# Late first stage: modulation steps moved into the feed-forward, convolution totals in place, taps and splits queued behind evacuations

## The chip, the cores and the metric

The kernel runs on one core of a Trainium2 chip. Its time is the device time of that core in microseconds. A core has TensorE (PE, matrix products), VectorE (DVE), ScalarE (ACT), GpSimd (POOL), SyncE (SP, whose queue issues the weight transfers here) and 16 DMA engines. Each engine works through a queue of its own in order; an instruction whose input or buffer is not ready holds up everything behind it on that engine.

## The reference

Two transformer blocks for 512 positions of width 1024, in fp32. The part that matters is the first block:

```python
h = rmsnorm(x, norm1_g)
z_glu, z_rx, z_rg, z_ga, z_gb = jnp.split(h @ w_in + b_in, split_idx, axis=-1)
u = z_glu[..., :1024] * sigmoid(z_glu[..., 1024:])
u = causal_depthwise_conv(u, conv_dw_w, conv_dw_b)           # 31 taps, 1024 channels
u = silu(layernorm(u, conv_ln_g, conv_ln_b))
y_a = u @ conv_w_out + conv_b_out
xb = causal_depthwise_conv(z_rx, lru_conv_w, lru_conv_b)     # 4 taps, 1280 channels
hb = rg_lru(xb, ...)                                         # gates, linear recurrence
y_b = (hb * gelu(z_rg)) @ lru_w_out
m = sigmoid(z_ga) * y_a + sigmoid(z_gb) * y_b
x = x + m @ w_mix_out
h = rmsnorm(x, norm2_g)
x = x + (silu(h @ ffn_w1) * (h @ ffn_w3)) @ ffn_w2           # then rmsnorm, then the second block
```

The second block starts from `mods = silu(c) @ w_ada + b_ada`: 9216 numbers from a 1024 x 9216 matrix, which depend on `c` alone and are first needed when the second block scales its input.

## The kernel before

Channels lie on the 128 partitions, the 512 positions along the free axis, so an activation is a list of tiles of 128x512. Every operand of a product is split into a high and a low fp32r part, and every product of a weight tile and an activation tile is three matmuls (`mm3`, L132 to L134: high x high, high x low, low x high). A weight block (512 KB, 128x1024) comes by DMA on SP's queue into one of 5 buffers `st`; ScalarE makes its high part `whi` (L125), VectorE or POOL its low part `wlo` (L126), 5 buffers each. Inside the first stage two of three low parts go to POOL. A product of 8 weight tiles (24 matmuls) is called a gemm below. Its result lies in one of 3 PSUM buffers `mm`; 5 more, `ax`, hold the accumulators of the convolution and small sums.

The program is a list of steps, each with its weights, a function and a slack, the time that its matmuls leave to the other engines. After each step, background work (`bg`) is queued until the slack is used up (`runbg`), and `defer(n, f)` queues `f` some gemms later. So the numbers of slack and cost decide where in the queues of VectorE and ScalarE a piece of background work stands. `tc.issue_after(x)` places instructions behind `x` in the queue.

The order of the first stage is written out: `g0 r0 r1 r2 r3 r4 g1 g2 a0 r5 a1 g3 a2 r6 a3 g4 a4 r7 r8 s0 g5 r9 b0 g6 b1 b2 g7 b3 b4`, then ten `q` with `s1`, then 8 `yb`, 8 `ga`, 8 `ya`, `mix`, and the feed-forward.

- `g` (`glu_step`): two gemms into `ga` (evacuated by ScalarE at L421) and `th` (evacuated at L430, multiplied at L431). The result is convolved in the background: 31 taps into two accumulators in PSUM, the first two by ScalarE (L401 to L404), 29 by VectorE (L406), then a total (L446, L447) and POOL's running sum `lnm` (L479).
- `r` (`rx_step`): a gemm into `rx` and the four taps `xb`. The steps g0 and r0 to r4 work on the input that is not yet normalised, so VectorE multiplies their results by the norm (`raw_z`, L395, tile `rx`) while `norm_h` makes the normalised input. Work that these steps leave behind is collected in the list `late`.
- `a`, `b` (`gate_step`): products of `xb`'s high and low parts `xbh`, `xbl` into the gates; `s`: the recurrence; `q` (`rg_step`): the gelu branch, whose product with the recurrence is split into `hbh`, `hbl`.
- `yb` (two products, 54 matmuls, from `hb` and the input), `ga` (one gemm), `ya` (one gemm on `u2h`, `u2l`, the normalised convolution).
- The layer norm is background work: `ln_mean` (sum of `lnm` over the partitions on TensorE, L196; VectorE makes `dg`, L217; TensorE spreads it, L224), `ln_var` (VectorE subtracts, L639; ScalarE squares, L251; VectorE sums into `lnv`, L252), `ln_rstd` (again L196, L217, L224), `ln_out` (L646, L647 and the splits `u2h`, `u2l`).

The modulation is 72 steps `ada_step`: a 512 KB DMA of `w_ada` into an `st` buffer and one VectorE operation over 128x1024 (L327) that sums a row into `mods`. Before, they stand behind every second `yb` (4), every `ga` (8), six of the `ya` and at places behind; the last runs at 761.55 us, and the first instruction that reads `mods` for the second block starts at 860.0 us.

## Time and profile before

| | us |
|---|---|
| median of 3 runs | 2270.68 (2270.66 to 2271.85) |
| the profiled execution | 2268.78 |
| its span, first to last instruction | 2267.1 |
| TensorE busy | 2207.7 (97%) |
| VectorE busy | 1401.8 (62%) |
| ScalarE busy | 941.8 (42%) |
| POOL busy | 159.3 (7%) |
| mean granted clock of TensorE | 0.991 of 2.4 GHz |

The span covers the time between the first and the last instruction; the profiled execution's own time is 1.7 us longer. TensorE is busy nearly everywhere, so what counts is where it is not: in the first 440 us, where the page's slices of its busy time fall to 9 and once to 6 tenths.

### The profile page before, as it was taken

How to read it: one execution, taken by the hardware profiler on the slowest of the kernel's cores; microseconds unless marked ns; L12 is line 12 of the kernel's file. 1: busy time of each engine (PE TensorE's matmuls, PEld its weight loads, DVE VectorE, ACT ScalarE, POOL GpSimd, SP SyncE). 2: the span in 40 equal slices, each digit the busy share in tenths (PEclk: the TensorE clock that was granted, in tenths of full speed). 3: DMA queues.
4: the chain of work that ended last, by engine and by line, in shares of the span. 5: the costliest groups of instructions: out<-in, count | busy, mean ns of one | idle time of the engine just before them, and what ended most of it. 6: DMA issues, size and time to landing. Idle time of an engine off the chain costs nothing.

```text
span 2267.1 us, 29984 instructions
## 1 busy us (share of the span) xinstructions
PE 2207.7 (97%) x11688; PEld 1888.2 (83%) x11688; DVE 1401.8 (62%) x2349; ACT 941.8 (42%) x1517; POOL 159.3 (7%) x179
## 2 busy tenths in 40 slices
PE   8899999699999999999999999999999999999997
PEld 6687788588888899988889987888888899988887
DVE  7999996768555448433325768675656558433334
ACT  6566433443222235322224567573433445322232
POOL 3334330000000000000100011000000000000000
PEclk9999999799999999999999999999999999999999
DMA  5433347245656534423234431213222323423342
GB/s 191 118 92 122 101 134 225 82 144 174 203 195 192 150 103 149 131 94 102 86 102 129 161 96 57 66 47 103 66 75 75 117 89 96 147 95 98 92 121 66
DMA packets 81438, 265.54 MB, mean 117 GB/s; under 512 B 10208, under 2 KB 12512, under 8 KB 81296
## 3 DMA queue, kind: packets, MB, share of 16 engines
q1 hardware_dynamic: 79888, 262.64, 36.8%
q8 instruction: 92, 1.51, 0.3%
q0 software_dynamic: 1264, 0.69, 0.1%
q14 instruction: 50, 0.41, 0.1%
q10 hardware_dynamic: 144, 0.29, 0.0%
HBM read 255.13 MB, written 4.19 MB: 114 GB/s over the span
## 4 chain that ended last, share of the span: by engine, by line
PE 81%; DVE 11%; issue 1%; ACT 1%; DMA 0%; POOL 0%; DVEq 0%; ACTq 0%; POOLq 0%
PE mm L132 24%; PE mm L133 24%; PE mm L134 24%; DVE ax L406 3%; DVE wlo L126 1%; PE ax L1231 1%; PE ax L1232 1%; PE ax L1233 1%; PE ax L1286 1%; PE ax L224 1%; PE ax L1415 1%; DVE xb L406 1%; PE ax L196 1%; DVE xb L567 1%; DMA st<-w_ada 0%
## 5 line engine op out<-in xcount | busy, mean ns | idle before, releaser
L125 ACT ACTIVATE whi<-st 128x1024 fp32r<-128x1024 f32 (+3 forms) x420 | 427.1, 1018 | 959.3 <-PE mm L133 594.4
L126 DVE TENSOR_TENSOR wlo<-st,whi 128x1024 fp32r<-128x1024 f32 (+3 forms) x378 | 454.1, 1202 | 415.8 <-ACT whi L125 414.7
L132 PE MATMUL mm<-pfh,whi 128*128 128x512 f32 (+1 forms) x1676 | 568.9, 339 | 0.5 <-ACT sq L251 0.5
L133 PE MATMUL mm<-pfl,whi 128*128 128x512 f32 (+1 forms) x1676 | 565.6, 338 | 0.0
L134 PE MATMUL mm<-pfh,wlo 128*128 128x512 f32 (+1 forms) x1676 | 564.4, 337 | 1.2 <-DVE wlo L126 1.2
L134 PEld LDWEIGHTS mm<-pfh,wlo 128*128 128x128 f32 x1676 | 316.8, 189 | 34.0 <-DVE wlo L126 1.9
L132 PEld LDWEIGHTS mm<-pfh,whi 128*128 128x128 f32 x1676 | 317.2, 189 | 33.5 <-ACT sq L251 1.4
L133 PEld LDWEIGHTS mm<-pfl,whi 128*128 128x128 f32 x1676 | 317.1, 189 | 31.7 <-issue 0.5
L132 PE MATMUL mm<-hi,whi 128*128 128x512 f32 x464 | 183.0, 394 | 10.4 <-ACT hi L354 6.2
L133 PE MATMUL mm<-lo,whi 128*128 128x512 f32 x464 | 183.4, 395 | 1.3 <-DVE lo L355 1.3
L134 PE MATMUL mm<-hi,wlo 128*128 128x512 f32 x464 | 182.4, 393 | 0.4 <-DVE wlo L126 0.4
L132 PE MATMUL mm<-mh,whi 128*128 128x256 f32 (+1 forms) x528 | 176.7, 335 | 2.2 <-ACT mh L852 1.1
L133 PE MATMUL mm<-ml,whi 128*128 128x256 f32 (+1 forms) x528 | 176.9, 336 | 0.0
L134 PE MATMUL mm<-mh,wlo 128*128 128x256 f32 (+1 forms) x528 | 176.4, 334 | 0.0
L406 DVE SCALAR_TENSOR_TENSOR ax<-th,d_hdw,ax 128x508 f32<-128x508 f32 (+27 forms) x232 | 157.7, 729 | 1.1 <-ACT ax L401 0.2
L133 PE MATMUL mm<-m1l,whi 128*128 128x512 f32 x368 | 143.3, 390 | 0.2 <-DVE m1l L686 0.2
L134 PE MATMUL mm<-m1h,wlo 128*128 128x512 f32 x368 | 143.0, 389 | 0.0
L132 PE MATMUL mm<-m1h,whi 128*128 128x512 f32 x368 | 143.0, 389 | 0.0
L327 DVE SCALAR_TENSOR_TENSOR st<-st,crow 128x1024 f32<-128x1024 f32 x72 | 88.5, 1229 | 73.6 <-DMA st<-w_ada 73.5
L865 DVE TENSOR_TENSOR fs<-fs,mm 128x512 f32<-128x512 f32 (+1 forms) x75 | 45.0, 600 | 128.0 <-PE mm L134 127.7
L132 PEld LDWEIGHTS mm<-hi,whi 128*128 128x128 f32 x464 | 88.1, 190 | 29.6 <-ACT hi L354 6.2
L132 PEld LDWEIGHTS mm<-mh,whi 128*128 128x128 f32 x528 | 100.1, 190 | 13.1 <-ACT mh L852 1.5
(363 smaller groups left out, 3319.2 us busy)
## 6 DMA issues: line engine op xcount, KB each, us to landing
st<-w_gu SPq DMA_DIRECT2D x102, 512.0 KB, 3.5
st<-w_ada SPq DMA_DIRECT2D x72, 512.0 KB, 4.0
st<-ffn_w SPq DMA_DIRECT2D x56, 512.0 KB, 3.6
st<-w_in SPq DMA_DIRECT2D x51, 512.0 KB, 4.0
st<-w2fm SPq DMA_DIRECT2D x51, 512.0 KB, 3.5
st<-w_dn SPq DMA_DIRECT2D x38, 448.0 KB, 3.3
st<-w_dn SPq DMA_DIRECT2D x24, 512.0 KB, 3.6
st<-w2v SPq DMA_DIRECT2D x16, 512.0 KB, 3.5
```

The costliest lines, as they stand in the source:

```text
L125: h = act(hi, src, AF.Copy)
L126: (eng or V).tensor_tensor(lo, src, hi, ALU.subtract)
L132: mm(out, whi, xh, start=start, stop=False)
L133: mm(out, whi, xl, start=False, stop=False)
L134: block[0] = mm(out, wlo, xh, start=False, stop=stop)
L196: mm(pc[:, i * nt + j:i * nt + j + 1], acc[:, r[0] + P * j:r[0] + P * (j + 1)], ones1, start=True, stop=True)
L224: mm(R[:, :nt * P], ones, dg.rearrange("p n t -> p (n t)"), start=True, stop=True)
L327: V.scalar_tensor_tensor(w, w, 1.0, crow, ALU.mult, ALU.mult, accum_out=mods[:, n:n + 1])
L406: V.scalar_tensor_tensor(acc[:, d:], u[:, :T - d], w, acc[:, d:], ALU.mult, ALU.add)
L567: V.tensor_tensor_scan(XB[j], GT[0, j], XB[j], 0.0, ALU.mult, ALU.add)
L865: V.tensor_tensor(s, s, rs(st["u"], r), ALU.mult)
L1231: mm(o, h[:, sl], hi[c], start=k == 0, stop=False)
```

## The change

Five things are changed, all in the program of the first stage and the feed-forward.

1. The modulation steps behind `yb` and `ga` (12) are gone from there. Two more stand behind `ya`, seven more in the first feed-forward (1.2 instead of 1.0 per weight pair's half) and three more in the product after it.
2. A convolution's total is written into the tile that was convolved (`u`, tile name `th`), not into a new one (`cv`).
3. First taps, totals and splits of ScalarE are queued behind the last evacuation of a PSUM buffer (`EV`), VectorE's taps behind the second last of certain multiplies (`DV`).
4. Of the work in `late`, three pieces are queued in the last `norm_h`, the rest behind the multiply of r4 (`raw_end`).
5. The last `hb` is split one gemm earlier, the layer norm's work waits for one step less, and in `yb` the background gets 1.15 times the slack.

```diff
--- before.py
+++ after.py
@@ -363,6 +363,7 @@
+    NEARLY = 3
     late = []
 
     def norm_h(m0):
@@ -380,19 +381,23 @@
                 h, l = H["h"][m]
                 H["h_last"] = V.tensor_tensor(l, ts[m - m0], h, ALU.subtract).ins
             if m0 + 2 == KT:
-                for f in late:
+                for f in late[:NEARLY]:
                     f()
-                late[:] = [None]
+                del late[:NEARLY]
         return fn
 
     def raw_end(W):
         del H["xg"], H["R"]
+        H["h_last"] = H["z_last"]
+        for f in late:
+            f()
+        late[:] = [None]
 
     def raw_z(W, t):
 
         ps = pmm()
         gemm(ps, W, H["xg"])
-        V.tensor_tensor(t, ps, H["R"], ALU.mult)
+        H["z_last"] = V.tensor_tensor(t, ps, H["R"], ALU.mult).ins
         return t
 
     def delay(acc, u, d, w, b, first=False):
@@ -407,6 +412,16 @@
 
     CV = [None] * KT
     EV = [None]
+    DV = [None, None]
+
+    def behind_ev():
+        return tc.issue_after(EV[0].ins) if EV[0] is not None else nullcontext()
+
+    def behind_dv():
+        return tc.issue_after(DV[0].ins) if DV[0] is not None else nullcontext()
+
+    def dv(ins):
+        DV[:] = [DV[1], ins]
 
     def glu_step(m, raw=False):
         st = {}
@@ -427,8 +442,8 @@
             else:
                 pg = pmm()
                 gemm(pg, W, H["h"])
-            act(u, pg, AF.Tanh, bias=dcol["hb_in"][:, 8 + m:9 + m], scale=0.5)
-            V.scalar_tensor_tensor(u, u, 1.0, st["a"], ALU.add, ALU.mult)
+            EV[0] = act(u, pg, AF.Tanh, bias=dcol["hb_in"][:, 8 + m:9 + m], scale=0.5)
+            dv(V.scalar_tensor_tensor(u, u, 1.0, st["a"], ALU.add, ALU.mult))
             cv = {}
 
             def taps(d0, d1):
@@ -438,12 +453,14 @@
                     for d in range(d0, d1):
                         w = dcol["hdw"][:, m * 31 + 30 - d:m * 31 + 31 - d]
                         acc = cv["p"][d % 2]
-                        delay(acc, u, d, w, col("conv_dw_b", m), first=d < 2)
+                        with behind_ev() if d < 2 else behind_dv():
+                            delay(acc, u, d, w, col("conv_dw_b", m), first=d < 2)
                 return f
 
             def total():
-                CV[m] = at(n="cv")
-                act(CV[m], cv["p"][0], AF.Copy)
+                CV[m] = u
+                with behind_ev():
+                    act(u, cv["p"][0], AF.Copy)
                 V.tensor_tensor(CV[m], CV[m], cv["p"][1], ALU.add)
 
             def convolve():
@@ -510,7 +527,9 @@
 
             def parts():
                 XBP[j] = (at(F32R, "xbh"), at(F32R, "xbl"))
-                split(xb, *XBP[j])
+                with behind_ev():
+                    act(XBP[j][0], xb, AF.Copy)
+                V.tensor_tensor(XBP[j][1], xb, XBP[j][0], ALU.subtract)
 
             def sides(m):
 
@@ -542,7 +561,7 @@
                 mm3(pg, hi[2 * q], lo[2 * q], *XBP[j], True, False)
                 mm3(pg, hi[2 * q + 1], lo[2 * q + 1], *XBN[j], False, True)
                 th = at(n="gt")
-                act(th, pg, AF.Tanh, bias=dcol[nmq][:, j:j + 1], scale=0.5)
+                EV[0] = act(th, pg, AF.Tanh, bias=dcol[nmq][:, j:j + 1], scale=0.5)
                 GT[q, j] = th
             r, ith = GT[0, j], GT[1, j]
             tt = at(n="tt")
@@ -551,7 +570,7 @@
             a2 = at(n="a2")
             GT[3, g] = act(a2, r, AF.Square)
             V.scalar_tensor_tensor(tt, a2, 1.0, tt, ALU.add, ALU.mult)
-            V.scalar_tensor_tensor(XB[j], ith, 1.0, XB[j], ALU.add, ALU.mult)
+            dv(V.scalar_tensor_tensor(XB[j], ith, 1.0, XB[j], ALU.add, ALU.mult))
             GT[2, j] = tt
         add([("w", I["lru_w"][j], 4, P)], fn, own=1.4)
 
@@ -578,12 +597,14 @@
             gemm(pz, W, H["h"])
             ge = at(n="ge")
             EV[0] = act(ge, pz, AF.Gelu_apprx_tanh, bias=col("b_in", 26 + j))
-            V.tensor_tensor(ge, ge, XB[j], ALU.mult)
+            dv(V.tensor_tensor(ge, ge, XB[j], ALU.mult))
 
             def parts():
                 HB[j] = (at(F32R, "hbh"), at(F32R, "hbl"))
-                split(ge, *HB[j])
-            defer(2, parts)
+                with behind_ev():
+                    act(HB[j][0], ge, AF.Copy)
+                V.tensor_tensor(HB[j][1], ge, HB[j][0], ALU.subtract)
+            defer(2 if j < NRNN - 1 else 1, parts)
         add(wunits("w_in", 26 + j, KT, [8]), fn, own=1.4)
 
     pool_steps = [0, 0]
@@ -594,10 +615,10 @@
             {"g": glu_step, "r": rx_step}[it[0]](n, raw=True)
             if it in ("r1", "r2", "r3"):
                 for m in {"r1": (0, 2), "r2": (4,), "r3": (6,)}[it]:
-                    add([], norm_h(m), own=2.9 + (12.0 if m == 6 else 0.0))
+                    add([], norm_h(m), own=2.9 + (5.0 if m == 6 else 0.0))
             if it == "r4":
                 pool_steps[0] = len(steps)
-                add([], raw_end)
+                add([], raw_end, own=7.0)
             continue
         {"g": glu_step, "r": rx_step, "q": rg_step, "s": scan_step, "a": lambda m: gate_step(0, m),
          "b": lambda m: gate_step(1, m)}[it[0]](n)
@@ -611,7 +632,7 @@
             pz = pmm()
             gemm(pz, W, H["h"])
             th = at(n="thb")
-            act(th, pz, AF.Tanh, bias=dcol["hb_in"][:, 44 + m:45 + m], scale=0.5)
+            EV[0] = act(th, pz, AF.Tanh, bias=dcol["hb_in"][:, 44 + m:45 + m], scale=0.5)
             st["th"] = th
 
         def fy(W):
@@ -622,8 +643,6 @@
 
         add(wunits("w_in", 44 + m, KT, [8]), fz)
         add(wunits("lru_w_out", m, NRNN, [5, 5]), fy, own=0.6)
-        if m % 2:
-            ada_step()
 
     U2 = []
 
@@ -649,7 +668,7 @@
         split(CV[m], *U2[m])
 
     def ln_push(W):
-        bg.extend([NEXT, NEXT])
+        bg.append(NEXT)
         later(0.9, ln_mean)
         for m in range(KT):
             later(1.4, lambda m=m: ln_var(m))
@@ -657,6 +676,7 @@
         for m in range(KT):
             later(1.4, lambda m=m: ln_out(m))
 
+    yb0 = len(steps)
     for m in range(KT):
         yb_step(m)
         if m == 0:
@@ -669,9 +689,8 @@
             pz = pmm()
             gemm(pz, W, H["h"])
             TA[m] = at(n="tha")
-            act(TA[m], pz, AF.Tanh, bias=dcol["hb_in"][:, 36 + m:37 + m], scale=0.5)
+            EV[0] = act(TA[m], pz, AF.Tanh, bias=dcol["hb_in"][:, 36 + m:37 + m], scale=0.5)
         add(wunits("w_in", 36 + m, KT, [8]), fn)
-        ada_step()
 
     def ya_step(m):
         def fn(W):
@@ -686,8 +705,7 @@
             V.scalar_tensor_tensor(lo, y, 0.5, hi, ALU.mult, ALU.subtract)
             M1.append((hi, lo))
         add(wunits("conv_w_out", m, KT, [8]), fn, own=2.1)
-        if m < 6:
-            ada_step()
+        ada_step()
 
     pool_steps[1] = len(steps)
     front = [len(steps)]
@@ -915,7 +933,7 @@
     add([], n2_end)
 
     def ada_between():
-        H["ada"] = H.get("ada", 0.0) + 1.0
+        H["ada"] = H.get("ada", 0.0) + 1.2
         while H["ada"] >= 1.0:
             H["ada"] -= 1.0
             ada_step()
@@ -1630,7 +1648,7 @@
         if any(a <= i < b for a, b in edges):
             runbg((slack - spent[0]) * 1.2)
         elif i < front[0]:
-            runbg(slack - spent[0])
+            runbg((slack - spent[0]) * (1.15 if i >= yb0 else 1.0))
         else:
             prep = sum(u[2] * u[3] / P * 0.143 for u in units if u[0] == "w")
             runbg((slack - prep) * (1.3 if ln_steps[0] <= i < ln_steps[1] else 1.0))
```

What this does to the queues, at three places. First, VectorE in r4: `rx` is the multiply of r4's result (561 or 553 are its numbers before and now), `xb` the taps of r2 to r4. Before:

```order
L406 SCALAR_TENSOR_TENSOR xb_391<-rx_390,pcol,xb_391 128x509
L406 SCALAR_TENSOR_TENSOR xb_460<-rx_459,pcol,xb_460 128x511
L406 SCALAR_TENSOR_TENSOR xb_504<-rx_503,pcol,xb_504 128x511
L406 SCALAR_TENSOR_TENSOR xb_460<-rx_459,pcol,xb_460 128x510
L406 SCALAR_TENSOR_TENSOR xb_504<-rx_503,pcol,xb_504 128x510
L406 SCALAR_TENSOR_TENSOR xb_460<-rx_459,pcol,xb_460 128x509
L406 SCALAR_TENSOR_TENSOR xb_504<-rx_503,pcol,xb_504 128x509
L395 TENSOR_TENSOR rx_559<-mm_561,R_249 128x512
L406 SCALAR_TENSOR_TENSOR ax_598<-th_319,d_hdw,ax_598 128x510
```

Now:

```order
L411 SCALAR_TENSOR_TENSOR xb_391<-rx_390,pcol,xb_391 128x509
L400 TENSOR_TENSOR rx_553<-mm_555,R_249 128x512
L411 SCALAR_TENSOR_TENSOR xb_460<-rx_459,pcol,xb_460 128x511
L411 SCALAR_TENSOR_TENSOR xb_504<-rx_503,pcol,xb_504 128x511
L411 SCALAR_TENSOR_TENSOR xb_460<-rx_459,pcol,xb_460 128x510
L411 SCALAR_TENSOR_TENSOR xb_504<-rx_503,pcol,xb_504 128x510
L411 SCALAR_TENSOR_TENSOR xb_460<-rx_459,pcol,xb_460 128x509
L411 SCALAR_TENSOR_TENSOR xb_504<-rx_503,pcol,xb_504 128x509
L411 SCALAR_TENSOR_TENSOR xb_554<-rx_553,pcol,xb_554 128x511
```

The multiply stands in front of the six taps of the tiles 460 and 504; before it stood behind them.

Second, ScalarE from g1's first evacuation on (`ga_619` or `ga_611`, g1's; `ga_720`, g2's; `th_674` or `th_662`, g1's second; `whi_749` and `whi_787` are weights). Before:

```order
L421 ACTIVATE ga_619<-mm_620,pcol 128x512
L125 ACTIVATE whi_749<-st_557 128x1024
L125 ACTIVATE xbh_670<-xb_560 128x512
L125 ACTIVATE whi_787<-st_596 128x1024
L430 ACTIVATE th_674<-mm_675,d_hb_in 128x512
L401 ACTIVATE ax_1047<-th_674,pcol,d_hdw 128x512
L421 ACTIVATE ga_720<-mm_721,pcol 128x512
L430 ACTIVATE th_755<-mm_756,d_hb_in 128x512
```

Now:

```order
L125 ACTIVATE whi_690<-st_501 128x512
L531 ACTIVATE xbh_654<-xb_504 128x512
L531 ACTIVATE xbh_658<-xb_554 128x512
L445 ACTIVATE th_662<-mm_663,d_hb_in 128x512
L125 ACTIVATE whi_749<-st_551 128x1024
L125 ACTIVATE whi_787<-st_596 128x1024
L436 ACTIVATE ga_720<-mm_721,pcol 128x512
L445 ACTIVATE th_755<-mm_756,d_hb_in 128x512
```

The evacuation into `th` stands in front of both weights, and the first tap (`ax`) that stood between `th` and `ga_720` is gone from there (`ax_598`'s, of g0, runs some rows earlier); `ga_720` is still behind `whi_787`.

Third, TensorE and VectorE at the layer norm. TensorE before, behind the last `ga` gemm (`mm_3254`):

```order
L133 MATMUL mm_3254<-lo_436,whi_3165 128x512
L134 MATMUL mm_3254<-hi_435,wlo_3166 128x512
L196 MATMUL ax_3281<-ones,lnm_1595 128x1 x4
L224 MATMUL ax_3290<-dg_3288,ones 128x512
L196 MATMUL ax_3326<-ones,lnv_3292 128x1 x4
L224 MATMUL ax_3348<-dg_3346,ones 128x512
L132 MATMUL mm_3404<-u2h_3352,whi_3205 128x512
```

Now, ahead of the fifth `ga` gemm and inside the seventh and eighth (two pieces):

```order
L133 MATMUL mm_3088<-lo_436,whi_2959 128x512
L134 MATMUL mm_3088<-hi_435,wlo_2960 128x512
L196 MATMUL ax_3115<-ones,lnm_1593 128x1 x4
L132 MATMUL mm_3151<-hi_421,whi_2963 128x512
L133 MATMUL mm_3151<-lo_422,whi_2963 128x512
```

```order
L134 MATMUL mm_3261<-hi_427,wlo_3047 128x512
L132 MATMUL mm_3261<-hi_429,whi_3046 128x512
L196 MATMUL ax_3219<-ones,lnv_3126 128x1 x4
L133 MATMUL mm_3261<-lo_430,whi_3046 128x512
L134 MATMUL mm_3261<-hi_429,wlo_3047 128x512
```

The sums of the layer norm now stand between matmuls of `ga`, the first 96 matmuls earlier than before; the last spreading (`ax_3241<-dg_3239`) stands 22 matmuls ahead of the end of `ga`. VectorE around the last total before (`cv_3241`), and now (`th_1675`):

```order
L327 SCALAR_TENSOR_TENSOR st_3303,mods<-st_3303,crow 128x1024
L126 TENSOR_TENSOR wlo_3249<-st_3169,whi_3248 128x1024
L327 SCALAR_TENSOR_TENSOR st_3437,mods<-st_3437,crow 128x1024
L126 TENSOR_TENSOR wlo_3399<-st_3209,whi_3398 128x1024
L327 SCALAR_TENSOR_TENSOR st_3479,mods<-st_3479,crow 128x1024
L126 TENSOR_TENSOR wlo_3441<-st_3252,whi_3440 128x1024
L447 TENSOR_TENSOR cv_3241<-cv_3241,ax_2949 128x512
L634 TENSOR_SCALAR s_3286<-ax_3281 128x4
```

```order
L411 SCALAR_TENSOR_TENSOR ax_2857<-th_1675,d_hdw,ax_2857 128x484
L411 SCALAR_TENSOR_TENSOR ax_2858<-th_1675,d_hdw,ax_2858 128x483
L411 SCALAR_TENSOR_TENSOR ax_2857<-th_1675,d_hdw,ax_2857 128x482
L126 TENSOR_TENSOR wlo_3047<-st_2917,whi_3046 128x1024
L464 TENSOR_TENSOR th_1675<-th_1675,ax_2858 128x512
L126 TENSOR_TENSOR wlo_3083<-st_2967,whi_3082 128x1024
L653 TENSOR_SCALAR s_3120<-ax_3115 128x4
L217 TENSOR_TENSOR dg_3122<-ident,s_3120 128x512
```

Before, the total stood behind modulation steps and low parts of weights; now it stands one low part behind the last tap.

## Rows read from the trace of the kernel before

**Rows 1.** The waits of TensorE up to 440 us. Columns: engine and line that waited, what it waited for, us in total, times, longest. (Those of the layer norm stand in rows 6.)

```profile
PE mm L132 <- ACT ga L421: 5.0, 2, 2.8
...
PE mm L132 <- DVE rx L395: 3.8, 1, 3.8
...
PE mm L133 <- DVE hbl L126: 2.3, 1, 2.3
PE mm L132 <- ACT th L430: 1.9, 2, 1.5
```

**Rows 2.** Busy time of each engine in stretches of 20 us: PE with its number of matmuls, weight loads, DVE, ACT, POOL, then the granted clock of TensorE, the share of the DMA engines and GB/s.

```profile
60.00:80.00 20.00, 16.25 (x65) 12.97 (x64) 19.92 (x29) 6.19 (x10) 5.26 (x4) 0.91 0.43 110
...
160.00:180.00 20.00, 17.23 (x71) 13.78 (x70) 20.00 (x29) 10.55 (x17) 6.26 (x4) 0.93 0.44 125
...
400.00:420.00 20.00, 5.01 (x12) 2.58 (x12) 15.05 (x33) 5.65 (x9) 0.00 (x0) 0.56 0.08 27
```

**Rows 3.** VectorE in order of time around the first stall: start, length, operation, count, and in brackets the idle time before it and what ended it.

```profile
55.89 11.20 DVE L406 SCALAR_TENSOR_TENSOR xb<-rx,pcol,xb 128x511 f32<-128x511 f32 x12
67.01 0.68 DVE L395 TENSOR_TENSOR rx<-mm,R 128x512 f32<-128x512 f32 x1
```

**Rows 4.** ScalarE in order of time at the second and third stall (same columns).

```profile
80.32 1.06 ACT L125 ACTIVATE whi<-st 128x1024 fp32r<-128x1024 f32 x1 [3.81 <-PE mm L133]
81.28 0.67 ACT L430 ACTIVATE th<-mm,d_hb_in 128x512 f32<-128x512 f32 x1
84.42 0.78 ACT L401 ACTIVATE ax<-th,pcol,d_hdw 128x512 f32<-128x512 f32 x1 [2.47 <-DVE th L431]
85.14 0.67 ACT L421 ACTIVATE ga<-mm,pcol 128x512 f32<-128x512 f32 x1
```

**Rows 5.** ScalarE in order of time at the fifth stall.

```profile
174.44 0.63 ACT L125 ACTIVATE xbh<-xb 128x512 fp32r<-128x512 f32 x1 [9.09 <-DVE xb L406]
```

**Rows 6.** TensorE in order of time: the first matmul behind the first stall, the first of the first and of the second `ga` gemm, the layer norm's four groups, the first of `ya`, and the first behind `ya`'s third gemm.

```profile
67.74 0.73 PE L132 MATMUL mm<-hi,whi 128*128 128x512 f32 x1 [3.75 <-DVE rx L395]
...
353.67 0.39 PE L132 MATMUL mm<-hi,whi 128*128 128x512 f32 x1
...
359.11 0.39 PE L132 MATMUL mm<-hi,whi 128*128 128x512 f32 x1
...
398.59 1.05 PE L196 MATMUL ax<-ones,lnm 128*128 128x1 f32 x8 [1.23 <-POOL lnm L479]
400.62 1.13 PE L224 MATMUL ax<-dg,ones 128*128 128x512 f32 x2 [0.98 <-DVE dg L217]
411.40 1.84 PE L196 MATMUL ax<-ones,lnv 128*128 128x1 f32 x8 [9.66 <-DVE lnv L252]
416.49 2.05 PE L224 MATMUL ax<-dg,ones 128*128 128x512 f32 x2 [3.25 <-DVE dg L217]
421.39 1.65 PE L132 MATMUL mm<-u2h,whi 128*128 128x512 f32 x3 [2.85 <-ACT u2h L125]
...
440.12 0.39 PE L132 MATMUL mm<-u2h,whi 128*128 128x512 f32 x1
```

**Rows 7.** VectorE in order of time: the last tap of the last convolution and the last total.

```profile
350.17 0.72 DVE L406 SCALAR_TENSOR_TENSOR ax<-th,d_hdw,ax 128x483 f32<-128x483 f32 x1
...
396.44 0.68 DVE L447 TENSOR_TENSOR cv<-cv,ax 128x512 f32<-128x512 f32 x1
```

**Rows 8.** VectorE by line from 354 to 397 us: busy us, mean ns of one, idle time before and what ended it.

```profile
L327 DVE SCALAR_TENSOR_TENSOR st<-st,crow 128x1024 f32<-128x1024 f32 x10 | 12.3, 1225 | 20.7 <-DMA st<-w_ada 20.7
L126 DVE TENSOR_TENSOR wlo<-st,whi 128x1024 fp32r<-128x1024 f32 x10 | 12.1, 1220 | 0.0
```

**Rows 9.** ScalarE in order of time near the end of `ga`.

```profile
391.72 1.06 ACT L125 ACTIVATE whi<-st 128x1024 fp32r<-128x1024 f32 x1 [3.80 <-PE mm L133]
...
393.26 0.59 ACT L446 ACTIVATE cv<-ax 128x512 f32<-128x512 f32 x1
```

**Rows 10.** VectorE in order of time inside the `yb` products: taps that alternate between two accumulators, and taps that stay on one.

```profile
281.15 5.18 DVE L406 SCALAR_TENSOR_TENSOR ax<-th,d_hdw,ax 128x497 f32<-128x497 f32 x8
...
339.97 3.82 DVE L406 SCALAR_TENSOR_TENSOR ax<-th,d_hdw,ax 128x497 f32<-128x497 f32 x5
```

**Rows 11.** VectorE by line from 280 to 352 us (columns as in rows 8).

```profile
L126 DVE TENSOR_TENSOR wlo<-st,whi 128x640 fp32r<-128x640 f32 (+1 forms) x8 | 12.7, 1591 | 0.0
```

**Rows 12.** VectorE in order of time beside a POOL operation.

```profile
149.72 0.68 DVE L566 TENSOR_TENSOR xb<-xb,tt 128x512 f32<-128x512 f32 x1
...
152.12 2.82 DVE L566 TENSOR_TENSOR xb<-xb,tt 128x512 f32<-128x512 f32 x1
```

**Rows 13.** POOL in order of time in the same stretch.

```profile
150.34 5.76 POOL L126 TENSOR_TENSOR wlo<-st,whi 128x1024 fp32r<-128x1024 f32 x2 [11.36 <-ACT whi L125]
```

**Rows 14.** VectorE in order of time in the first feed-forward: a modulation step and the sixth after it.

```profile
601.07 1.23 DVE L327 SCALAR_TENSOR_TENSOR st<-st,crow 128x1024 f32<-128x1024 f32 x1 [3.30 <-DMA st<-w_ada]
...
631.96 1.23 DVE L327 SCALAR_TENSOR_TENSOR st<-st,crow 128x1024 f32<-128x1024 f32 x1 [1.55 <-DMA st<-w_ada]
```

**Rows 15.** The waits of all engines from 560 to 760 us (columns as in rows 1).

```profile
ACT whi L125 <- PE mm L133: 69.4, 20, 3.9
...
DVE st L327 <- DMA st<-w_ada: 39.6, 32, 3.5
```

**Rows 16.** POOL in order of time: the last running sum of the convolution.

```profile
397.27 1.27 POOL L479 TENSOR_TENSOR lnm<-lnm,cv 128x512 f32<-128x512 f32 x1 [27.63 <-DVE cv L447]
```

## The prediction

> **What bounds the kernel now.** I read the waits of TensorE first, because it is the busiest engine by far: up to 440 us it waits in two places beside the start, and behind that seldom for more than 1 us. Then I read the windows, to see what those waits cost beside themselves, and last each waiting place engine by engine.
>
> The first place is the early stage. TensorE waits six times: 3.8 us for VectorE's multiply in r4, 5.0 us in two waits and 1.9 us in two for ScalarE's evacuations `ga` and `th`, 2.3 us for `hbl` [rows 1]. That is 13.0 us. The whole loss there is larger. TensorE could go on at 67.74 − 3.75 = 63.99 us and begins `ga` at 353.67; by the program 1200 matmuls lie between. 24 of them take 359.11 − 353.67 = 5.44 us [rows 6], so 1200 take 272.0 us, and 289.7 were needed: 17.7 us lost. The 4.7 us beyond the waits lie mostly behind them: the granted clock is 0.91 in the window of the first stall and 0.93 in that of the fifth, of 2.4 GHz [rows 2].
>
> The second place is the layer norm. `ga` is over at 353.67 + 8 × 5.44 = 397.2 us; then TensorE does four small groups, each behind a wait (1.23, 0.98, 9.66, 3.25, and 2.85 us for the first `u2h`), and three gemms of `ya` end at 440.12 [rows 6]. Twelve records of matmuls fall into 400 to 420 us, at a clock of 0.56 [rows 2]. Undisturbed, the 42.9 us would be 72 × 0.2267 = 16.3 us for `ya` and, at most, twice 1.05 + 1.13 = 4.4 us for the groups (I take the two that ran before the long wait). So 22.2 us are lost. Both places together hold 39.9 us, and that is the most that the change can give.
>
> **Why each stall is there, and what the change does to it.**
>
> *First stall.* VectorE works on twelve `xb` taps from 55.89 for 11.20 us, and the multiply that frees r4's PSUM buffer comes behind them at 67.01 [rows 3]. Now it stands behind six. Half of 11.20 us ends at 61.5, or 62.5 if the slow ones are in front; the multiply takes 0.68, so it ends by 63.2 at the latest, and TensorE needs it at 63.99. 3.75 us become 0; the six taps behind it are needed only by a0, several us later.
>
> *Second and third.* ScalarE's in-order queue holds them: `whi` waits 3.81 us for TensorE to free its buffer and the evacuation `th` stands behind it until 81.28; a first tap waits 2.47 us for VectorE and `ga` stands behind it until 85.14 [rows 4]. Now `th` stands ahead of both weights and the tap is gone. One evacuation is still behind a weight that waits for the gemm that TensorE is just finishing: that gemm's end, 1.06 for the weight and 0.67 for the evacuation make it 1.7 us late, and TensorE has by then about 1.3 us of gate products left (6 × 0.2267). 0.4 us remain of 3.7.
>
> *Fifth.* `xbh` waits 9.09 us for r9's taps, which VectorE interleaves with other taps until 174.4, and `ga` waits behind it [rows 5]. Now `xbh` is queued behind the evacuation, and those taps stand some 20 us earlier. 0 remain; so too for `hbl`, whose split is one gemm earlier. So 17.3 of the 17.7 us should go, the clock's share with the gaps that precede it.
>
> *Layer norm.* The last tap is done at 350.9, but the last total only at 396.44 [rows 7]: ten modulation steps stand before it, 12.3 us of work with 20.7 us of waiting for `w_ada` [rows 8], and ScalarE's half of it stands behind a weight that waits 3.80 us for TensorE [rows 9]. With these steps gone the total's time is set by two chains, both counted from the end of `yb`. VectorE: by the new order one multiply (0.7), 20 taps at 5.18 / 8 = 0.65 (they now alternate between accumulators; on one accumulator it was 0.76) [rows 10], four low parts at 1.2 [rows 8], total 0.7, POOL's sum 1.3 [rows 16]: 20.5 us. ScalarE: the third `ga` gemm ends at 16.3, then weight, evacuation and copy as in rows 9 (2.2), total, POOL: 20.5 us too. With some 0.4 for handing over, 21 us; TensorE reaches the first group behind four gemms, at 21.8. It doesn't wait, with 0.8 us to spare. Then, as the old trace has it [rows 6]: from the first group to `dg` 2.0 us, and seven matmuls (1.6) lie between: 0.4 lost. From there to `lnv` 400.62 to 411.40 = 10.8, plus two low parts that stand between (2.4), against 54 matmuls (12.2) and the group's own 1.1: nothing. From `lnv` to `dg` 5.1 against 13 matmuls and the group (2.9 + 1.05): 1.1 lost. From `dg` to the first `u2h` 4.9, in which the table load of SiLU (which was earlier) can hide behind the spreading, against 22 matmuls (5.0): nothing; and `ya` eats a `u2h` per 1.36 us (6 × 0.2267), the old trace makes one every 1.2. I allow 0.5 for it. 2.0 us stay of 22.2.
>
> *What is added.* Behind the first stage the twelve steps return: two at `ya`, seven in the feed-forward, three behind it. I cost them at nothing. There each step is a DMA and 1.23 us of VectorE in one circulating buffer; the steps come every (631.96 − 601.07) / 6 = 5.15 us [rows 14], and VectorE waits for them. But ScalarE's `whi` waits 69.4 us of the 200 for TensorE [rows 15], which waits for no weight there: the weights are some four gemms ahead. Below nothing it can't go, since no wait is there to be won; the other bound is a rival. `mods` is complete at 763.6 us now and first read at 860.0; three more products put it near 779. The in-place total costs nothing: the copy waits for the last tap, which it needed anyway.
>
> **Sum.** 17.3 + 20.2 = 37.5 us at most. ScalarE's new queueing can make small waits that the old trace doesn't show. Bounds: nothing, or all six old ones in other places (17.7). I take one of mean size, (13.0 + 4.7) / 6 = 2.9. 34.6 us saved on the profiled execution's 2268.8 gives 2234.2; the median was 1.9 above it: **2236 us**.
>
> **Rivals.**
>
> *VectorE falls behind in `yb`* (0.17). A period there is 54 matmuls, 12.24 us. VectorE has up to 15 taps (9.7), one low part at 1.59 as measured there [rows 11], one multiply (0.6): 11.9, and 11.2 in every second one. That is tight. While POOL made low parts from 150.34 to 156.1 [rows 13], the same VectorE operation took 2.82 instead of 0.68 us [rows 12]. One such operation more per period would be 2.1 us; the periods would need 13.7, and over eight VectorE comes 11 us late to the last total, TensorE waits 10 of them: 2246. Against it: the old mean of 1.59 already holds such cases. The Trainium skill (SBUF — State Buffer, "Who interferes with whom") states it as a rule: a VectorE instruction with two SBUF inputs and a GpSimd one that reads SBUF exclude each other, one with a single SBUF input is not touched. The trace agrees, 2.82 against 0.68. By the rule the taps, which read one input from PSUM, go on, and only the low part can be hit.
>
> *Half of it stays.* If the early waits come back in other places in full, the saving is 2.9 + 20.2 − 5.5 = 17.6 to 20.2: 2250 to 2253 (0.08). If the layer norm stays outside `ga` because its first sum comes late by more than a gemm, 20.2 is lost instead: 2256 (0.06).
>
> *Modulation becomes the bound of the feed-forward* (0.05). 45 steps at 5.15 us are 231.8 us, the 38 products at 5.44 are 206.7. If the steps keep to one buffer, TensorE loses 25 us: 2261. Against it: two steps in a row take two of the five buffers.
>
> *Slower* (0.06). ScalarE's total waits in the queue for VectorE's last tap, and `thb` and the weights stand behind it. If VectorE is behind throughout, each of eight convolutions stops TensorE once. From 34.6 / 8 = 4.3 us each it eats the whole gain; at twice that the time is 2305. Against it: the old kernel had the same copy in the same queue and TensorE had no wait on it [rows 1].
>
> *No effect* (0.03): the saved waits are paid elsewhere one for one, 2270.
>
> **Numbers.** My own case, 2229 to 2242, has 0.55. The low end is all 39.9 us won. The range 2228 to 2253 adds the late VectorE and the early waits, 0.8 in all. Faster by over 0.2% (4.5 us, about what a measurement here can tell) is everything but the last two and a share of noise: 0.90; within 0.04; slower 0.06.
>
> **What would show it.** Right: TensorE's waits for `rx`, `ga`, `th`, `hbl` gone or below 1 us; the group on `lnm` between `ga` gemms, at about 358 us; `ya` beginning near 386 and directly behind `ga`; windows up to 420 us with 88 to 90 matmuls; no wait for a weight between 420 and 780 us. Wrong: a wait of many us for `lnm`, long waits of ScalarE for VectorE's taps ahead of `thb`, or waits for `whi` and `wlo` in the feed-forward.

## The result, and the profile after

The median is 2234.71 us (2233.5 to 2238.4) against 2271.26 for the kernel before on the same chip, 36.6 us less: ratio 0.9842, 95% interval 0.9825 to 0.9859. The forecast was 2236, the range 2228 to 2253. The profiled execution took 2235.89 us, 32.9 less than the profiled one of before. The two differences disagree because the profiled execution of before was 2.5 us faster than its median, and this one is 1.2 us slower than its own.

TensorE's waits up to 440 us in the changed kernel (columns as in rows 1):

```profile
PE mm L132 <- ACT hi L354: 6.2, 1, 6.2
PE mm L132 <- ACT m1h L704: 1.8, 2, 1.3
PE mm L133 <- DVE lo L355: 1.6, 5, 0.5
PE mm L132 <- ACT gt L564: 0.9, 1, 0.9
PE mm L133 <- DVE m1l L705: 0.6, 1, 0.6
PE mm L133 <- DVE u2l L126: 0.4, 2, 0.2
```

The first and the third belong to the start and were there before. All four lines of [rows 1] are gone, and all the layer norm's but 0.4 us; one of 0.9 us for a gate is new, and one at `m1h` and `m1l`, the start of the mix products. The windows (columns as in rows 2):

```profile
60.00:80.00 20.00, 19.86 (x88) 16.13 (x87) 20.00 (x25) 13.96 (x23) 10.18 (x7) 1.00 0.46 116
160.00:180.00 20.00, 19.14 (x85) 15.53 (x84) 19.29 (x25) 12.71 (x22) 8.26 (x6) 1.00 0.47 142
400.00:420.00 20.00, 20.00 (x90) 16.57 (x89) 18.38 (x27) 8.81 (x12) 0.00 (x0) 1.00 0.83 290
```

Where [rows 2] showed 65, 71 and 12 matmuls at clocks of 0.91, 0.93 and 0.56, there are 88, 85 and 90, all at 1.00. The layer norm's groups on TensorE, from the first `ga` gemm on:

```profile
337.59 0.39 PE L132 MATMUL mm<-hi,whi 128*128 128x512 f32 x1
...
359.35 0.95 PE L196 MATMUL ax<-ones,lnm 128*128 128x1 f32 x8
...
375.13 1.02 PE L196 MATMUL ax<-ones,lnv 128*128 128x1 f32 x8
379.31 1.12 PE L224 MATMUL ax<-dg,ones 128*128 128x512 f32 x2
385.28 0.39 PE L132 MATMUL mm<-u2h,whi 128*128 128x512 f32 x1
```

None waits; in [rows 6] each did, by up to 9.66 us. But the first group has little to spare: TensorE arrives behind four gemms at 337.59 + 21.76 = 359.35, and POOL's sum, which it needs, ended 0.3 us earlier. VectorE and POOL at that place:

```profile
356.07 0.68 DVE L464 TENSOR_TENSOR th<-th,ax 128x512 f32<-128x512 f32 x1
356.67 1.22 DVE L126 TENSOR_TENSOR wlo<-st,whi 128x1024 fp32r<-128x1024 f32 x1
356.89 2.14 POOL L496 TENSOR_TENSOR lnm<-lnm,th 128x512 f32<-128x512 f32 x1 [26.53 <-DVE th L464]
```

In [rows 16] the sum took 1.27 us; now VectorE makes a low part of a weight from 356.67 to 357.89 beside it.

Where the time went, from the first matmul of three places in both traces. Before, the mix products began at 467.32 and ended at 511.38:

| | before | after | saved in all | forecast |
|---|---|---|---|---|
| `ga` begins | 353.67 | 337.59 | 16.1 | 17.3 |
| mix begins (`ya` done) | 467.32 | 429.78 | 37.5 | 37.5 |
| mix ends | 511.38 | 476.67 | 34.7 | 34.6, behind the 2.9 allowed for new waits |

The 37.5 us at the start of mix agree with the forecast because two misses cancel: the early stage saved 1.2 us less than forecast, and the layer norm 1.2 us more.

Through the rest of the first feed-forward nothing changes (its remaining products start 34.7 us earlier and end 34.7 us earlier). Near the end the profiled execution gives back 1.8 us. Most of that lies at one place, 1848 us, and it is TensorE's clock. TensorE has the same three waits there in both kernels (0.83, 1.11 and 0.28 us before, 0.84, 1.11 and 0.28 now), but behind them the granted clock falls to 0.50 (1.2 GHz) in the changed kernel and stays at 1.00 (2.4 GHz) in the kernel before. Equal lengths of time behind the third wait, first now, then before (columns as in rows 2):

```profile
1848.49:1851.90 3.41, 3.41 (x19) 3.41 (x17) 3.41 (x10) 1.82 (x4) 0.00 (x0) 0.50 0.00 0
```

```profile
1883.44:1886.85 3.41, 3.41 (x31) 3.41 (x30) 3.41 (x10) 1.82 (x4) 0.00 (x0) 1.00 0.00 0
```

In the changed kernel 19 matmuls fall into it, before 31, and half of 3.41 us is 1.7 us. The second run of the changed kernel (`again` below) shows the same fall from 1847.02 to 1850.43 us, while the kernel with part 1 undone has the same waits and keeps 1.00. Why the clock falls in one and not in the other is not shown; a difference of 1 to 2 us between two versions can come from this place alone.

### The profile page after: what moved, and what is told of

Same layout as the page of the kernel before. It is cut to its first block, busy times and chain, and to the rows that moved or that the text cites. A ratio compares the mean times of both kernels' runs of the same rounds, so it can differ in the third digit from the quotient of the medians.

```text
span 2234.2 us, 29966 instructions
## 1 busy us (share of the span) xinstructions
PE 2201.8 (99%) x11688; PEld 1884.4 (84%) x11688; DVE 1400.2 (63%) x2349; ACT 941.3 (42%) x1517; POOL 156.3 (7%) x179
## 4 chain that ended last, share of the span: by engine, by line
PE 89%; DVE 6%; ACT 2%; issue 1%; DMA 1%; SPq 0%; DVEq 0%; ACTq 0%
PE mm L132 27%; PE mm L133 27%; PE mm L134 26%; PE ax L1249 1%; PE ax L1251 1%; PE ax L1250 1%; DVE wlo L126 1%; PE ax L1304 1%; PE ax L224 1%; PE ax L1433 1%; PE ax L196 1%; DMA st<-w_ada 0%; ACT p L1417 0%; ACT whi L125 0%; DVE s L1416 0%
## 5 line engine op out<-in xcount | busy, mean ns | idle before, releaser
L126 DVE TENSOR_TENSOR wlo<-st,whi 128x1024 fp32r<-128x1024 f32 (+2 forms) x378 | 454.6, 1204 | 372.6 <-ACT whi L125 371.6
L411 DVE SCALAR_TENSOR_TENSOR ax<-th,d_hdw,ax 128x510 f32<-128x510 f32 (+28 forms) x232 | 154.2, 728 | 0.0
L134 PEld LDWEIGHTS mm<-mh,wlo 128*128 128x128 f32 x528 | 100.8, 191 | 10.0
```

The lines of the kernel that those rows point to most:

```text
L126: (eng or V).tensor_tensor(lo, src, hi, ALU.subtract)
L134: block[0] = mm(out, wlo, xh, start=False, stop=stop)
L411: V.scalar_tensor_tensor(acc[:, d:], u[:, :T - d], w, acc[:, d:], ALU.mult, ALU.add)
```

## Experiments

Five kernels undo one part each, and one makes part 1 alone in the kernel before. The edits are shown shortened; `...` stands for lines left out.

**Part 1 undone: modulation back in `yb` and `ga`.**

```diff
+        if m % 2:                                   # behind yb
+            ada_step()
...
+        ada_step()                                  # behind ga
...
-        ada_step()                                  # behind ya
+        if m < 6:
+            ada_step()
...
-        H["ada"] = H.get("ada", 0.0) + 1.2
+        H["ada"] = H.get("ada", 0.0) + 1.0
```

> The changed kernel with part 1 alone undone: modulation steps again behind every second yb, every ga and six ya, 1.0 per weight pair's half in the feed-forward. By its order the first group of the layer norm (on lnm) still comes inside ga (122 matmuls behind its start instead of 96), the second (on lnv) only behind ga. Theory (the modulation steps in front of the last total are what holds the layer norm back): TensorE loses the two chains lnv to dg (4.1 us) and dg to u2h (3.7 us) and some waiting for lnm or lnv, with the low clock behind it 9 to 14 us, and wins back the 2.8 us that it loses in the mix products of the changed kernel: about 2243 us (2240 to 2247), with waits of over 2 us on lnv, dg and u2h and none above 1 us up to ga. Rival (the stage's order and the queueing alone hide the layer norm): 2232 to 2236. Second rival (all of the old loss of 22 us comes back): 2254.

Measured: 2249.5 us, 0.9905 (0.9888 to 0.9922). That is 15 us lost, 2.5 us above the upper end of what was expected (2247). The expected wait on `lnv` did not come; most of the loss lies in the chain from `lnv` to `dg`, which I had put at 4.1 us. TensorE:

```profile
364.81 0.95 PE L196 MATMUL ax<-ones,lnm 128*128 128x1 f32 x8
382.54 1.02 PE L196 MATMUL ax<-ones,lnv 128*128 128x1 f32 x8
396.61 2.07 PE L224 MATMUL ax<-dg,ones 128*128 128x512 f32 x2 [13.05 <-DVE dg L217]
401.54 1.65 PE L132 MATMUL mm<-u2h,whi 128*128 128x512 f32 x3 [2.85 <-ACT u2h L125]
```

The modulation steps do hold the last total back, as said: it begins at 361.61, 24.5 us behind the begin of `ga` at 337.15, and in the changed kernel 18.5 us behind it. But TensorE does not wait for it, because the group on `lnm` stands 26 matmuls later here (122 instead of 96): POOL's sum ended at 364.65, 0.2 us ahead of the group. What costs time is the small chain behind `lnv`, a dozen VectorE instructions of 0.16 us for the square root, of which nine now stand behind a step or a low part:

```profile
361.61 0.69 DVE L464 TENSOR_TENSOR th<-th,ax 128x512 f32<-128x512 f32 x1
...
383.60 0.16 DVE L232 TENSOR_SCALAR s<-ax 128x4 f32<-128x4 f32 x1
383.68 1.22 DVE L327 SCALAR_TENSOR_TENSOR st<-st,crow 128x1024 f32<-128x1024 f32 x1
384.82 0.16 DVE L206 TENSOR_SCALAR s<-s 128x4 int32<-128x4 int32 x1
384.90 1.22 DVE L126 TENSOR_TENSOR wlo<-st,whi 128x1024 fp32r<-128x1024 f32 x1
```

From the group on `lnv` to the spreading of `dg` 14.1 us pass instead of 4.2 in the changed kernel. And the start of the mix products has no wait here: it comes with the moved steps.

**Part 3 undone: no queueing behind evacuations.**

```diff
-        return tc.issue_after(EV[0].ins) if EV[0] is not None else nullcontext()
+        return nullcontext()
...
-        return tc.issue_after(DV[0].ins) if DV[0] is not None else nullcontext()
+        return nullcontext()
```

> The changed kernel with part 3 alone undone: first taps, totals and splits of ScalarE and the taps of VectorE stand where the background queues them, not behind an evacuation. Theory (the early waits for th, ga and xbh came from ScalarE's work in front of the evacuations): waits of TensorE on ScalarE's evacuations of 1.5 to 3 us come back up to 180 us, 6 us in all with the low clock behind them 6 to 9; the wait on rx (3.8 us) stays away; the layer norm stays hidden: 2241 to 2244 us. Rival (the queue rules matter little once the late work is split): 2233 to 2237.

Measured: 2252.2 us, 0.9912 (0.9897 to 0.9927), 17 us lost where 6 to 9 were expected. TensorE waits 7.9 us for `ga` in two pieces and 2.8 us for `ge`; the layer norm stays hidden, and the wait on `rx` stays away. ScalarE around the longest:

```profile
171.07 0.63 ACT L531 ACTIVATE xbh<-xb 128x512 fp32r<-128x512 f32 x1 [11.30 <-DVE xb L411]
171.60 1.04 ACT L125 ACTIVATE whi<-st 128x1024 fp32r<-128x1024 f32 x1
172.55 0.67 ACT L436 ACTIVATE ga<-mm,pcol 128x512 f32<-128x512 f32 x1
```

It is the picture of [rows 5], the evacuation behind a split that waits for VectorE's taps, only 11.3 us instead of 9.1. The mechanism is as said; the size was not: the waits are 2.95, 4.98 and 2.84 us, where 1.5 to 3 were expected. 10.7 us of waiting cost 17 us because the clock falls with each; the windows of the first two (columns as in rows 2):

```profile
80.00:100.00 20.00, 20.00 (x83) 16.36 (x82) 20.00 (x30) 12.71 (x19) 6.72 (x4) 0.91 0.47 145
160.00:180.00 20.00, 15.02 (x54) 11.85 (x53) 20.00 (x31) 5.74 (x9) 6.33 (x6) 0.83 0.40 118
```

In the second window there are 54 matmuls for 90; the wait of 5.0 us stands for 22 of them. The granted clock is 0.50 from 80.21 to 83.62, from 172.4 to 179.2 and from 237.2 to 240.6 us, each time in or right behind one of the waits. In these 13.6 us TensorE is busy for 12.3, which at the full clock would have taken half: some 6 us beside the 10.7.

**Part 4 undone: all late work in the last `norm_h`.**

```diff
-                for f in late[:NEARLY]:
+                for f in late:
                     f()
-                del late[:NEARLY]
+                late[:] = [None]
...
-        H["h_last"] = H["z_last"]
-        for f in late:
-            f()
-        late[:] = [None]
...
```

> The changed kernel with part 4 alone undone: all the late work is queued in the last norm_h, so twelve xb taps stand in front of the multiply of r4 again. Theory: the wait on rx of 3.8 us comes back with 1.7 us of low clock, nothing else changes: 2239 to 2241 us. Rival (VectorE, which no longer has as much in front of it, is early enough): 2234 to 2236.

Measured: 2244.25 us, 0.9877 (0.9863 to 0.9892), some 9 us lost, 3 more than expected. The wait that was expected is back to the hundredth, and another with it:

```profile
67.50 0.50 PE L132 MATMUL mm<-hi,whi 128*128 128x512 f32 x1 [3.75 <-DVE rx L396]
82.33 0.50 PE L132 MATMUL mm<-xbh,whi 128*128 128x512 f32 x1 [2.02 <-ACT th L441]
```

The second is the late `th` of [rows 4]: one more split stands between the waiting weight and the evacuation. So parts 3 and 4 both guard that place.

**Part 5 undone: the pace of the background.**

```diff
-            defer(2 if j < NRNN - 1 else 1, parts)
+            defer(2, parts)
...
-        bg.append(NEXT)
+        bg.extend([NEXT, NEXT])
...
-            runbg((slack - spent[0]) * (1.15 if i >= yb0 else 1.0))
+            runbg((slack - spent[0]) * 1.0)
```

> The changed kernel with part 5 alone undone: last hb split two gemms late, layer norm two steps late, background in yb at 1.0 of the slack. By its order the first group of the layer norm stands behind 168 matmuls of ga instead of 96, the second behind ga. Theory: the modulation steps were needed but are not enough, the pace decides how much of the chain lies inside ga; exposed are then what is left of dg to lnv (10.8 us against 18 matmuls, 4.1), lnv to dg (4.1) and dg to u2h (3.7), so 12 to 16 us more: 2247 to 2251 us. Rival (moving the modulation steps is what hides the layer norm): 2234 to 2238.

Measured: 2252.4 us, 0.9917 (0.9903 to 0.9932), 17 to 18 us lost, 1.4 us above the upper end of what was expected (2251). TensorE:

```profile
375.26 0.95 PE L196 MATMUL ax<-ones,lnm 128*128 128x1 f32 x8
390.71 1.84 PE L196 MATMUL ax<-ones,lnv 128*128 128x1 f32 x8 [8.04 <-DVE lnv L252]
399.86 2.05 PE L224 MATMUL ax<-dg,ones 128*128 128x512 f32 x2 [7.32 <-DVE dg L217]
404.76 1.65 PE L132 MATMUL mm<-u2h,whi 128*128 128x512 f32 x3 [2.85 <-ACT u2h L125]
```

The modulation steps are out of `ga` here, and still most of the chain lies behind it. Which of the three numbers of part 5 does it was not tested.

**Part 2 undone: totals in a tile of their own.**

```diff
-                CV[m] = u
+                CV[m] = at(n="cv")
                 with behind_ev():
-                    act(u, cv["p"][0], AF.Copy)
+                    act(CV[m], cv["p"][0], AF.Copy)
```

> The changed kernel with part 2 alone undone: a convolution's total goes into a tile of its own again. By its order every group of the layer norm stands where it stood. Theory (the total in place moves no instruction of weight and costs nothing): the same as the changed kernel beside it within 1 us. Rival (the eight tiles more make activations wait for a free tile): waits of TensorE on ScalarE or VectorE of several us, 2238 to 2245.

Measured: 2235.7 us, 0.9835 (0.9819 to 0.9851), beside 2234.6 and 0.9834 (0.9819 to 0.9848) for the changed kernel itself. No difference can be told. The losses of the other four undone parts add up to some 60 us, more than the 36.6 gained: the parts are not separate gains.

**The changed kernel again, as the measure beside those runs.**

> The changed kernel again, on the chip of the runs beside it: 2233 to 2238 us. No theory hangs on it; it is the measure for the runs beside it.

Measured: 2234.6 us, as said.

**Part 1 alone, in the kernel before.**

```diff
-        if m % 2:                                   # behind yb
-            ada_step()
...
-        ada_step()                                  # behind ga
...
-        if m < 6:                                   # behind ya
-            ada_step()
+        ada_step()
...
-        H["ada"] = H.get("ada", 0.0) + 1.0
+        H["ada"] = H.get("ada", 0.0) + 1.2
```

> The kernel before with part 1 alone: the modulation steps moved, all else as it was. By its order the first group of the layer norm stands behind 168 matmuls of ga (before: 192) and the second still behind ga, as in the changed kernel without part 5. Theory (part 1 makes room for the layer norm, but only the pace of part 5 moves it into ga, and the early waits have nothing to do with part 1): the early waits on rx, ga and th stay, 12 to 13 us of waiting; at the layer norm waits on lnv of about 8 us, on dg of 4 to 7 and on u2h of 3 stay; 4 to 7 us are saved: 2264 to 2268 us beside a kernel before of 2272. Rival (the modulation steps were what held the layer norm; with them gone it hides): 20 us less, 2252.

Measured: 2267.9 us, 0.9980 (0.9971 to 0.9989): 5 us saved, as the theory had it. Its longest waits, without those of the start:

```profile
PE ax L196 <- DVE lnv L252: 9.1, 1, 9.1
PE mm L132 <- ACT ga L421: 5.0, 2, 2.8
PE mm L132 <- DVE rx L395: 3.8, 1, 3.8
PE ax L224 <- DVE dg L217: 3.2, 1, 3.2
PE mm L132 <- ACT u2h L125: 2.9, 1, 2.9
```

So neither moving the steps nor the pace hides the layer norm alone: 5 us for the one, and 15 to 18 that are lost when either is missing.

Five kernels take up the new wait at the mix products, and how much modulation the feed-forward takes.

**No steps behind `ya`, and 1.42 or 1.6 per half pair in the feed-forward.**

```diff
         add(wunits("conv_w_out", m, KT, [8]), fn, own=2.1)
-        ada_step()
...
-        H["ada"] = H.get("ada", 0.0) + 1.2
+        H["ada"] = H.get("ada", 0.0) + 1.42     # 1.6 in the second kernel
```

> The changed kernel without modulation steps behind ya (8 there); the feed-forward has 1.42 of them per weight pair's half instead of 1.2 (53 or 54 instead of 45). Theory (in the changed kernel the steps behind ya crowd VectorE and the DMA queue: the first one can run only when ScalarE has made the silu of c, at 392 us behind the layer norm's, and four weight buffers wait for it; so m1h is late at the start of the mix products, 2.8 us with the clock): the waits on m1h and m1l go, and the feed-forward stays free of waits: 2.3 to 3 us less than the changed kernel beside it. Rival (the mix products wait because of the layer norm's end or of ya's own work, not of the steps): 0 to 0.5 us less. Second rival (the feed-forward has no room for eight more): slower than the changed kernel by 10 us or more.

> As the kernel without steps behind ya, but 1.6 per weight pair's half in the feed-forward, so 60 or 61 steps there, and fewer in the product behind it. It presses on the rival of the prediction that the steps become the bound of the feed-forward: at one buffer and 5.15 us a step, 60 steps are 309 us and the 38 products 206.7, so 100 us more. Theory (a second step in a row takes another buffer, and ScalarE's weights are four products ahead): the steps come every 3.4 us, no wait of TensorE on a weight in the feed-forward, and the time is that of the kernel without steps behind ya within 0.5 us. If the truth is between, waits for whi or wlo of TensorE between 520 and 720 us show how much.

Measured: 2246.6 us with 1.42 (0.9886, 0.9871 to 0.9900), 12 us more than the changed kernel; 2238.0 with 1.6 (0.9848, 0.9833 to 0.9862), some 3 us more. The waits at `m1h` and `m1l` fall to 0.2 us in both, so the steps behind `ya` have to do with them; mix takes 44.4 and 44.2 us, 46.9 in the changed kernel and 45.8 in its second run `again`. What is won there is lost again in the feed-forward and more, some 15 us with 1.42, and in a way that no theory had. TensorE's waits from 460 to 760 us, none in the changed kernel, with 1.42 and with 1.6:

```profile
PE mm L132 <- DVE fs L882: 11.2, 8, 2.1
```

```profile
PE mm L132 <- DVE fs L882: 2.8, 1, 2.8
```

It isn't weights that are missing. VectorE, in order, with 1.42:

```profile
602.36 1.22 DVE L327 SCALAR_TENSOR_TENSOR st<-st,crow 128x1024 f32<-128x1024 f32 x1 [1.75 <-DMA st<-w_ada]
603.51 1.22 DVE L126 TENSOR_TENSOR wlo<-st,whi 128x1024 fp32r<-128x1024 f32 x1
607.84 1.23 DVE L327 SCALAR_TENSOR_TENSOR st<-st,crow 128x1024 f32<-128x1024 f32 x1 [3.11 <-DMA st<-w_ada]
608.99 0.68 DVE L882 TENSOR_TENSOR fs<-fs,mm 128x512 f32<-128x512 f32 x1
```

and SP's queue in the same stretch:

```profile
595.92 2.06 SPq L1578 DMA_DIRECT2D st<-w_ada  x2
603.62 0.33 SPq L1578 DMA_DIRECT2D st<-w_ada  x1
609.10 2.06 SPq L1578 DMA_DIRECT2D st<-w_ada  x2
```

A transfer starts 0.1 us behind the end of a modulation step (603.51, 608.99), lands about 4 us later, its step waits for it, and the evacuation `fs`, which frees TensorE's PSUM buffer, stands behind that step. Three steps to two products make a round of 609.10 − 595.92 = 13.2 us, and two products are 10.9. The transfers themselves are not at their limit: from 520 to 720 us they move 211 GB/s with 1.42 and 236 with 1.6, where the steps are more and the waits fewer. Why the pattern of 1.6 goes more smoothly I did not settle.

**A sixth weight buffer for the kernel with 1.42.**

```diff
-    NA = 67
-    NST, NHI, NLO = 5, 5, 5
-    LA_D, LA_P = 4, 4
+    NA = 66
+    NST, NHI, NLO = 6, 5, 5
+    LA_D, LA_P = 5, 4
...
-        return sp.tile([P, 8], dt, tag="s", bufs=24, name=nm(n))[:, :w]
+        return sp.tile([P, 8], dt, tag="s", bufs=12, name=nm(n))[:, :w]
```

> The kernel without modulation steps behind ya and 1.42 of them per half pair in the feed-forward, with six weight buffers st instead of five and transfers issued one weight further ahead; for the room, one activation tile and half of the small tiles fewer. Without the sixth buffer it lost 15 us to its wait-free sibling in the feed-forward: VectorE waited for w_ada there, and with it everything behind it, the evacuation fs that TensorE needs. Theory (the waits come from five buffers in rotation: a transfer of w_ada can start only when the buffer's last user is done, and that is often a modulation step): VectorE's wait for w_ada falls to below half of 84 us, TensorE's wait on fs goes below 3 us, and as the mix products don't wait either the time is 2231 to 2235 us beside 2272. Rival (the transfers themselves are too slow for 5 blocks per two products, or VectorE's order alone makes the wait): fs waits of about 11 us stay, 2244 to 2248 us.

Measured: 2276.8 us, 1.0020 (1.0011 to 1.0029). The wait on `fs` falls from 11.2 to 5.5 us and VectorE's wait for `w_ada` from 83.8 to 75.3, far less than the theory wanted, and the kernel is 30 us slower than the one without the sixth buffer, most of it behind the first feed-forward. I put that down to the tiles given up for the buffer, which is not shown. The run speaks against the buffers as the whole cause, but with several sizes changed at once it decides nothing.

**Four steps behind `ya` instead of eight, the other four in the mix products.**

```diff
-        ada_step()
+        if m >= 4:                                  # m % 2 in the second kernel
+            ada_step()
...
-            if 1 < m < 6:
-                ada_step()                          # mix
+            ada_step()
```

> The changed kernel with modulation steps behind the last four ya alone (four instead of eight) and behind all eight mix products (eight instead of four); the feed-forward as in the changed kernel, 1.2. Theory (steps that stand behind the first ya block four weight buffers until the silu of c is made, and crowd VectorE later; the mix products have room, VectorE being busy for 69% of 440 to 460 us; the feed-forward's pattern is what it was): the waits on m1h and m1l at the start of mix go below 0.5 us, 1.5 to 2.5 us less than the changed kernel: 0.9825 of the kernel before, 2232 to 2233 us beside 2272. Rival (four steps behind the last ya crowd VectorE as much): no difference.

> The same with the four steps behind every second ya (the second, fourth, sixth and eighth). Theory: VectorE has time to catch up between two steps, but the first two still hold weight buffers until 392 us: the waits on m1h and m1l half as long, 0.5 to 2 us less than the changed kernel. Rival (only the number of steps counts): the same as with the four steps behind the last ya.

Measured: 2236.2 us (0.9838, 0.9824 to 0.9851) and 2235.5 (0.9838, 0.9825 to 0.9852): no gain by either. The waits at the start of mix stay, 2.3 and 2.6 us beside 2.4 in the changed kernel. Behind them the granted clock is 0.5 for 3.4 us (from 437.95 and from 437.2 us), which the changed kernel's two profiles do not show, and mix takes 48.0 and 48.1 us. VectorE with the late four:

```profile
434.22 0.69 DVE L702 TENSOR_TENSOR ya<-ya,thb 128x512 f32<-128x512 f32 x1
435.82 1.22 DVE L327 SCALAR_TENSOR_TENSOR st<-st,crow 128x1024 f32<-128x1024 f32 x1 [0.92 <-DMA st<-w_ada]
436.98 0.69 DVE L705 SCALAR_TENSOR_TENSOR m1l<-ya,m1h 128x512 fp32r<-128x512 f32 x1
```

The step stands in front of `m1l` of the last `ya`, which TensorE waits for, and itself waits for its transfer. By the order it is the twelfth: a mix product's step depends on nothing in that product, so the scheduler puts all eight of them ahead of this place, behind the four of `ya`. In the changed kernel twelve stand there too (eight and four), with every second `ya` twelve again, and without steps behind `ya` four. In the kernel before it was four as well: the six of `ya` ran ahead of the layer norm. So moving steps from `ya` to mix moved nothing. My theory that the first steps' blocked buffers were to blame falls, the rival that only their number counts stands. No version here beats the changed kernel.

## Why the prediction was right, step by step

The mechanisms of the two large terms came as said, and 36.6 us less is near the 34.6 of the sum. That 2236 and 2234.7 lie so close is partly luck. Misses of 1.2 us in the early stage and at the layer norm cancel, a cost of 2.8 us at mix fell on an allowance of 2.9 us made for something else, and the 1.9 us by which I put the median above the profiled execution has nothing to do with the change: here the median lies 1.2 us below it.

- **First stall.** 3.75 us to 0, as said; the undone part brings back 3.75.
- **Second, third, fifth, `hbl`.** Gone as said. The 0.4 us that I left at the second gates did not come, but a wait of 0.9 us for a gate at 167.45 did, which I had not placed. The early stage saves 16.1 us, 1.2 less than the sum had.
- **Layer norm.** 20.2 us forecast, 37.5 − 16.1 = 21.4 measured. The two chains to the last total were read rightly (the copy by ScalarE ended at 356.0, 18.4 us behind the begin of `ga`; 16.3 + 2.2 = 18.5 was worked out), but POOL's sum took 0.9 us more than its row, more than the whole margin of 0.8. Only because handing over took less than the 0.4 us allowed were 0.3 us left, which is luck again. The Trainium skill (SBUF — State Buffer, "Who interferes with whom") states that a VectorE instruction with two SBUF inputs and a GpSimd instruction that reads SBUF exclude each other. The trace agrees: POOL's sum took 2.14 us beside VectorE's low part of a weight, 1.27 alone. I weighed that rule only for VectorE being slowed.
- **Reason for the old loss.** I said that modulation steps held the last total. In the order before they did [rows 7, 8], and with part 1 undone they hold it by 6.0 us again; but what TensorE waits for there, 13.05 us, is a second hold, the small square-root chain, that I did not see, and the run with part 1 alone shows that without the pace the same chain stays outside. The sum held because both parts came together.
- **What is added, at nothing.** This is the step that failed. In the feed-forward the cost is nothing in time (no wait of TensorE from 460 to 760 us), though more than half of the cover is gone. From 560 to 760 us, in the changed kernel:

```profile
DVE st L327 <- DMA st<-w_ada: 80.9, 38, 3.6
ACT whi L125 <- PE mm L133: 28.9, 12, 3.8
```

  In [rows 15] ScalarE waited 69.4 us for TensorE and VectorE 39.6 for `w_ada`. At `ya`, twelve steps now stand between the layer norm and the last `m1l`, since none can run before the late SiLU of `c` (made at 392 us); before, it was four. They cost 46.9 − 44.1 = 2.8 us of mix in the profiled execution, and 45.8 − 44.1 = 1.7 in `again`. The allowance of 2.9 us for small new waits had its size by luck; I had put it on ScalarE's queueing in the early stage, where 1.2 us came.
- **Rivals.** VectorE did not fall behind in `yb`. The modulation rival did not come at 45 steps. In the kernel with about 53 steps in the feed-forward it is real but of another kind, not by weights but by the evacuation behind a waiting step; and it is not the number alone, since 60 steps lost less (2.8 us of waiting on `fs` instead of 11.2).
- **Two bounds that do not follow from the sum.** All 39.9 us won would give 2270.7 − 39.9 = 2230.8, not 2229: the 1.9 us of the median are missing there. And for the early waits coming back in full the sum gives 37.5 − 17.7 = 19.8 us saved; the 2.9 + 20.2 − 5.5 used instead is not derived. Neither changes the forecast.

## What to carry to other kernels

An instruction that waits for a transfer must not stand on an in-order engine in front of an evacuation that the matrix engine needs; a step that depends on nothing is put there by a scheduler without warning, so look in the order for what stands ahead of the last consumer. When a serial chain is to lie inside other work, count every short instruction in it: twelve of 0.16 us took 14.1 us instead of 4.2 when nine of them got a long neighbour. Parts that look like separate gains can need each other: here moving the filler saved 5 us alone, and its absence cost 15.
